# Output projection in token groups of 800 and 256 instead of 704 and 352, the first group's rows kept in DRAM until their norm, outputs on two queues

## The chip, the core and the metric

The kernel runs on one core of a Trainium2 chip. A core has five engines that run their own instruction streams and meet at semaphores: TensorE (PE; its weight loads are listed as PEld), VectorE (DVE), ScalarE (ACT), GpSimd (POOL) and SyncE (SP). SyncE, ScalarE and GpSimd can issue DMA transfers, and an engine whose next instruction is a transfer that has to wait holds up everything behind it on that engine. Data lies in DRAM, in SBUF (128 partitions) and in PSUM, eight banks into which TensorE accumulates.

The metric is the device time of one execution in microseconds (us). Three timed runs of the kernel before gave 1811.63, 1812.21 and 1813.61 us.

## The reference

One layer of a decoder trunk for 1024 prompt tokens and 32 sample tokens (8 sequences of 4), 1056 tokens together, with 2048 features:

```python
xn = rms_norm(x, norm_w)
proj = xn @ w_in                       # split into the inputs of four branches
...
mix = jnp.concatenate([y_ml, y_ssd, y_sc, y_rg], axis=-1)
y = x + mix @ w_out                    # (tokens, 2048) @ (2048, 2048)
...
y_prompt = rms_norm(yp, final_norm_w)  # y * rsqrt(mean(y*y) + EPS) * final_norm_w
y_sample = rms_norm(ys, final_norm_w)
```

All is float32. The change concerns the last two steps, the output projection with its residual and the final norm.

## The kernel before

Features lie on partitions, tokens along the free axis. The 2048 features are 16 tiles of 128 (`KT`), so an output tile `n` is 128 features by a number of tokens.

**Products.** Each float32 operand is split into a high part rounded to the fast matmul format and the rest. `mm6` (line 276) does, for each of the two 128-row slices of a weight pair, three matmuls into one bank: high by high, high by low, low by high (lines 281 to 283). A weight pair is 128 x 256 floats, 128 KiB in DRAM. It is loaded by SyncE into a raw buffer (`w_load`, line 251), ScalarE writes the high part (line 262), VectorE the rest (line 263). In the output projection there are six raw buffers, and a load into one waits for the split that read it last. There are four buffers for split pairs and, in the second token group, four more that lie in `xl`. `w_next` hands out the next split pair, frees the one before it, splits as many as there are free buffers, and loads as many as there are free raw buffers.

**Order.** The program order of each engine is that of the Python code. Work beside the main loop runs in generators on two lanes; `tick()`, called once for each weight pair, lets each lane go one step, and a generator that yields 4 is called again four ticks later. SBUF outside the fixed tiles is one arena, `take` and `drop` give and return areas, and an area that was returned may be handed out at once: whatever then writes it waits for the last reader.

**Output projection (`out_proj`).** The tokens go through in two groups, `GA` and `GB`: 704 tokens as two chunks of 352, then the last 352. In each group all 16 output tiles are computed, so all weights of `w_out` are read twice. The first four tiles of group one go weight by weight through all eight banks, since the inputs still arrive; after that a tile uses two banks of four. `begin(n, gr)` loads the residual x for the tile on SyncE (line 1339). `fin(n, gr, banks)` adds the bank to it (VectorE, line 1349), squares it (ScalarE, 1356) and adds the square to the running sum `acc` (GpSimd, or VectorE for the last two tiles, 1357). In group two it also multiplies by the final norm's weight (1359).

**Final norm of group one (`finish`).** All 16 tiles of group one stay in SBUF, 16 x 704 floats a partition. When the group is done, `finish` is put on a lane and runs beside the second group: `row_rsqrt` turns `acc` into the reciprocal root for each token, spread over the partitions, and then every four ticks a tile is multiplied by it (VectorE, 1452) and written out by GpSimd (1453).

**The end.** After the last matmul of group two the sums over features are made by small matmuls (1421, 1426), roots and reciprocals follow, the reciprocals are spread by transposes (1432), and the 16 tiles are multiplied, eleven by VectorE from PSUM (1441), four by GpSimd (1439), the last by VectorE (1437). SyncE issues all 16 output transfers (1442).

Of the kernel before, what the change touches and what calls it, by code (L numbers as in the profile page):

```python
# [9 lines left out]
F32 = mybir.dt.float32  # L10
# [3 lines left out]
OP = mybir.AluOpType  # L14

D = 2048
KT = 16
TP = 1024
TS = 32
NT = TP + TS  # L20
# [3 lines left out]
NEG = -1e30  # L24
KSC = 128.0 ** -0.5
SLOT = 1084
GA = (CH, CH)
GB = CH
WARM = 12
CM = max(*GA, GB)  # L30

# [77 lines left out]
class Build:  # L109
    def __init__(self, ctx, tc, io):  # L110
        self.tc, self.nc, self.io = tc, tc.nc, io
        nc = tc.nc
        self.V, self.S, self.G, self.P, self.Q = nc.vector, nc.scalar, nc.gpsimd, nc.tensor, nc.sync
        main = ctx.enter_context(tc.tile_pool(name="main", bufs=1))
        psum = ctx.enter_context(tc.tile_pool(name="psum", bufs=1, space=bass.MemoryType.PSUM))
        dram = ctx.enter_context(tc.tile_pool(name="dram", bufs=1, space=bass.MemoryType.DRAM))
        ctx.enter_context(tc.manual_schedule())
        self.xh = main.tile([128, KT, NT], F32R, name="xh")
        self.xl = main.tile([128, KT, NT], F32R, name="xl")
        self.NRAW, self.NW = 3, 4  # L120
        self.wbuf = {}
        self.wraw = deque(main.tile([128, 2, 128], F32, name=f"wr{i}") for i in range(self.NRAW))
        self.whl = deque((main.tile([128, 2, 128], F32R, name=f"wh{i}"), main.tile([128, 2, 128], F32R, name=f"wl{i}"))
                         for i in range(self.NW))
        self.wcur = {}
        self.fa = main.tile([128, 1040], F32R, name="fa")
        self.fb = main.tile([128, 256], F32R, name="fb")
        na = 15290
        self.ar = Arena(main.tile([128, na], F32, name="arena"), na)
        self.bank = [psum.tile([128, 512], F32, name=f"bank{i}") for i in range(8)]  # L130
        self.npj = self.nmx = 0
        self.mixd = dram.tile([KT, 128, NT], F32, name="mixd")
        self.rowd = dram.tile([24, NT], F32, name="rowd")
        self.nrmd = dram.tile([4, NT], F32, name="nrmd")
        self.lanes = [deque(), deque()]
        self.wait = [0, 0]
        self.ready = {}
        self.land = {}
        self.held = False
# [1180 lines left out]
    def out_proj(self):  # L1320
        V, S, G, P, Q = self.V, self.S, self.G, self.P, self.Q
        io = self.io
        W = [sum(GA), GB]
        T0 = [0, W[0]]
        acc = [self.take(W[0]), None]
        ys = [{}, {}]
        sq = [self.take(CM) for i in range(2)]
        nacc = [0, 0]
        nsq = 0
        pairs = lambda ap: ap.rearrange("p (k m) -> p k m", k=2)  # L1330
        for _ in range(3):
            self.wraw.append(pairs(self.take(256).ap))

        def begin(n, gr):
            if gr:
                ys[1][n] = self.take_tick(GB).ap
            else:
                ys[0][n] = self.ar.take(W[0])
            Q.dma_start(ys[gr][n][:, :], io["x"][:, n, T0[gr] + 1:T0[gr] + W[gr] + 1])

        def fin(n, gr, banks):

            nonlocal nsq
            y, a = ys[gr][n], acc[gr]
            o = 0
            nacc[gr] += 1
            for b, w in banks:
                ts = slice(o, o + w)
                V.tensor_add(y[:, ts], b[:, :w], y[:, ts])  # L1349
                o += w  # L1350
                if nacc[gr] == 1:
                    S.activation(a[:, ts], y[:, ts], AF.Square)
                else:
                    t = sq[nsq % 2][:, :w]
                    nsq += 1
                    S.activation(t, y[:, ts], AF.Square)  # L1356
                    (G if nacc[gr] < KT - 1 else V).tensor_add(a[:, ts], a[:, ts], t)  # L1357
                if gr:
                    S.activation(y, y, AF.Copy, scale=self.par("fnorm", n))

        def chunks(gr):
            t = T0[gr]
            out = []
            for w in (GA if gr == 0 else (GB,)):
                out.append((self.pj(), t, w))
                t += w
            return out

        def mm(ch, ke, w):
            for b, t, n in ch:  # L1370
                self.mm6(b, *w, ke, t, n, ke == 0, ke == 7)


        first = [chunks(0) for _ in range(2)] + [[(self.bank[b + i], sum(GA[:i]), w) for i, w in enumerate(GA)] for b in (4, 6)]
        for ke in range(8):
            for n in self.FIRST:
                mm(first[n], ke, self.w_next())
                k = 2 * ke + 6 + n // 2
                if n % 2:
                    if k + 4 < KT:  # L1380
                        self.mix_load(k + 4)
                    if k < KT:
                        self.mix_split(k)
                if ke == 5:
                    begin(n, 0)
                self.tick()
        for n in self.FIRST:
            fin(n, 0, [(b, w) for b, _, w in first[n]])
        self.states_out()
        for n in range(4, KT):  # L1390
            begin(n, 0)
            ch = chunks(0)
            for ke in range(8):
                mm(ch, ke, self.w_next())
                self.tick()
            fin(n, 0, [(b, w) for b, _, w in ch])
        acc[1] = self.take(GB).ap
        self.lanes[0].append(self.finish(acc[0], ys[0]))

        for i in range(4):  # L1400
            self.whl.append((self.xl[:, 2 * i:2 * i + 2, 128:256], self.xl[:, 2 * i + 8:2 * i + 10, 128:256]))
        for n in range(KT):
            begin(n, 1)
            ch = chunks(1)
            for ke in range(8):
                mm(ch, ke, self.w_next())
                self.tick()
            if n == KT - 1:
                break
            fin(n, 1, [(b, w) for b, _, w in ch])  # L1410

        nb = (GB + 127) // 128
        cut = [(i, slice(128 * i, min(GB, 128 * i + 128)), min(128, GB - 128 * i)) for i in range(nb)]
        tc, rc, mean = self.take(nb), self.take(nb), self.take(2)
        V.memset(mean.ap, 1.0 / D)
        V.memset(tc.ap, 1.0)
        S.activation(rc[:, 0:1], tc[:, 0:1], AF.Sqrt)
        bs, bk = [self.mx() for _ in cut], self.pj()
        y, t, b = ys[1], sq[0], ch[0][0]
        for i, ts, m in cut:  # L1420
            P.matmul(bs[i][:m, 0:1], acc[1][:, ts], mean[:, 0:1], start=True, stop=False)
        for ts in (slice(0, 128), slice(128, GB)):
            V.tensor_add(y[KT - 1][:, ts], b[:, ts], y[KT - 1][:, ts])
            S.activation(t[:, ts], y[KT - 1][:, ts], AF.Square)
        for i, ts, m in cut:
            P.matmul(bs[i][:m, 0:1], t[:, ts], mean[:, 0:1], start=False, stop=True)
        for i, ts, m in cut:
            S.activation(tc[:m, i:i + 1], bs[i][:m, 0:1], AF.Sqrt, bias=self.eps[:m])
        V.reciprocal(rc.ap, tc.ap)
        bk2 = self.pj()  # L1430
        for b, (i, ts, m) in [(b, x) for b in (bk, bk2) for x in cut]:
            P.transpose(b[:, ts], rc[:m, i:i + 1].to_broadcast([m, 128]), self.ident[:m, :m])
        rb = self.take(GB)
        S.activation(rb.ap, bk2[:, :GB], AF.Copy)
        for n in range(KT):
            if n == KT - 1:
                V.scalar_tensor_tensor(y[n], y[n], self.par("fnorm", n), rb.ap, op0=OP.mult, op1=OP.mult)
            elif n % 3 == 2 and n < 14:
                G.tensor_mul(y[n], y[n], rb.ap)
            else:  # L1440
                V.tensor_mul(y[n], y[n], bk[:, :GB])
            Q.dma_start(io["y_out"][n, :, W[0]:NT], y[n])

    def finish(self, acc, ys):

        w = acc.n
        yield 4
        rb = self.fa[:, :w].bitcast(F32)
        yield from self.row_rsqrt(acc, w, 1.0 / D, EPS, rb, 3, True)
        for n in range(KT):  # L1450
            y = ys[n]
            self.V.scalar_tensor_tensor(y.ap, y.ap, self.par("fnorm", n), rb, op0=OP.mult, op1=OP.mult)
            self.G.dma_start(self.io["y_out"][n, :, 0:w], y.ap)
            if n:
                ys[n - 1].drop()
            yield 4
        ys[KT - 1].drop()

    def states_out(self):
        G, io = self.G, self.io  # L1460
# [122 lines left out]
```

## Time and profile before

| | |
|---|---|
| median of the timed runs | 1812.21 us |
| the profiled execution | 1812.29 us |
| its span, first to last instruction | 1810.1 us |
| mean granted TensorE clock | 0.995 |
| TensorE busy, weight loads busy | 99%, 97% of the span |
| VectorE, ScalarE, GpSimd busy | 50%, 29%, 10% |
| read from and written to DRAM | 144.35 MB, 21.84 MB |
| first token group's matmuls | to about 1672 us |
| second group's matmuls | to 1795.8 us |

An execution takes about 2.2 us more than its span. In rows that group instructions, the line is followed by engine, operation, output<-inputs, shape and count; behind the bar stand the busy us, the mean ns of one, and the idle us of the engine just before them with what ended them. In the view by windows, each engine's busy us and number of instructions stand for a stretch of the run, then the granted clock, the DMA engines' busy share and GB/s. In the view in order of time a row gives its start in us, its length and how many instructions it merges. Transfer rows give the KiB of one and the median us from issue to landing; in the rows of the DMA queues, q1 is SyncE's queue and q0 GpSimd's, followed by packets, MB, and the share of the sixteen DMA engines' time.

### The profile page before, as it was taken

Reading aid. Unit: us, or ns where it says so; the run is one execution under the profiler, and the core shown is the slowest. Engines: PE = TensorE matmul, PEld = TensorE weight load, DVE = VectorE, ACT = ScalarE, POOL = GpSimd, SP = SyncE. Lnnn points to the kernel's source line nnn. Section 1 sums busy time; section 2 is a strip of 40 time slices with the busy share of each in tenths; the row PEclk is TensorE's granted clock in tenths of the full one; section 3 lists DMA queues with packets and bytes.
Section 4 is the critical chain, followed back from the end, with each engine's and each line's share of the span. In section 5 each row is a group of like instructions: output and inputs, shape, how many; then the busy total and the mean of one; then the engine's idle time right before and its main releaser. Section 6 shows DMA issues by size and latency. Waiting matters only on the chain.

```text
span 1810.1 us, 30156 instructions
## 1 busy us (share of the span) xinstructions
PE 1788.5 (99%) x11459; PEld 1755.0 (97%) x11459; DVE 909.0 (50%) x2018; ACT 529.9 (29%) x1263; POOL 178.8 (10%) x243
## 2 busy tenths in 40 slices
PE   9999999999999999999999999999999999999997
PEld 7899999999999999989999999999999999999997
DVE  4484544625435444764267647543773543333664
ACT  5522222212212111321144212311441432222453
POOL 1000102011011000320000003100000011110121
PEclk9999999999999999999999999999999999999998
DMA  9411213222122112332211224221213633333774
GB/s 321 161 51 50 77 49 91 50 73 71 58 68 62 55 56 71 94 76 81 61 45 57 62 65 107 66 84 53 62 56 95 201 109 99 92 91 87 212 244 153
DMA packets 141557, 168.17 MB, mean 93 GB/s; under 512 B 18220, under 2 KB 126196, under 8 KB 140900
## 3 DMA queue, kind: packets, MB, share of 16 engines
q1 hardware_dynamic: 135492, 145.36, 28.5%
q0 software_dynamic: 5184, 19.42, 2.8%
q8 instruction: 89, 1.46, 0.3%
q10 hardware_dynamic: 736, 1.48, 0.3%
q14 instruction: 56, 0.46, 0.1%
HBM read 144.35 MB, written 21.84 MB: 92 GB/s over the span
## 4 chain that ended last, share of the span: by engine, by line
PE 91%; DMA 4%; DVE 2%; issue 1%; ACT 1%; POOL 1%; SPq 1%; DVEq 0%; POOLq 0%; ACTq 0%
PE bank L281 29%; PE bank L283 29%; PE bank L282 28%; DMA arena<-rowd 3%; POOL arena L1074 1%; DMA wr<-in_w_in 1%; DVE arena L1083 0%; DMA arena<-in_x 0%; DVE wl L263 0%; PE bank L898 0%; PE bank L494 0%; PE bank L876 0%; PE bank L897 0%; PE bank L900 0%; ACT wh L262 0%
## 5 line engine op out<-in xcount | busy, mean ns | idle before, releaser
L281 PE MATMUL bank<-xh,wh 128*128 128x352 f32 x3328 | 1085.6, 326 | 1.4 <-ACT xh L470 0.9
L282 PE MATMUL bank<-xl,wh 128*128 128x352 f32 x3328 | 1072.8, 322 | 2.0 <-DVE xl L473 1.9
L283 PE MATMUL bank<-xh,wl 128*128 128x352 f32 x3328 | 1072.9, 322 | 0.7 <-DVE wl L263 0.5
L281 PEld LDWEIGHTS bank<-xh,wh 128*128 128x128 f32 x3328 | 626.0, 188 | 14.4 <-issue 9.9
L282 PEld LDWEIGHTS bank<-xl,wh 128*128 128x128 f32 x3328 | 626.8, 188 | 3.0 <-DVE xl L473 3.0
L283 PEld LDWEIGHTS bank<-xh,wl 128*128 128x128 f32 x3328 | 626.6, 188 | 2.0 <-DVE wl L263 2.0
L263 DVE TENSOR_TENSOR wl<-wr,wh 128x256 fp32r<-128x256 f32 x537 | 233.1, 443 | 397.9 <-ACT wh L262 397.5
L262 ACT ACTIVATE wh<-wr 128x256 fp32r<-128x256 f32 x537 | 214.6, 412 | 585.4 <-PE bank L282 483.6
L591 DVE TENSOR_TENSOR arena<-bank,arena 128x352 f32<-128x352 f32 x114 | 58.8, 524 | 80.1 <-PE bank L283 79.7
L263 DVE TENSOR_TENSOR wl<-arena,wh 128x256 fp32r<-128x256 f32 x103 | 43.7, 442 | 61.0 <-ACT wh L262 60.9
L1357 POOL TENSOR_TENSOR arena<-arena 128x352 f32<-128x352 f32 x39 | 36.9, 950 | 314.0 <-ACT arena L1356 208.5
L942 DVE SCALAR_TENSOR_TENSOR arena<-arena 128x1080 f32<-128x1080 f32 (+1 forms) x44 | 59.9, 1361 | 1.0
L262 ACT ACTIVATE wh<-arena 128x256 fp32r<-128x256 f32 x103 | 40.3, 410 | 65.4 <-PE bank L282 62.1
L1356 ACT ACTIVATE arena<-arena 128x352 f32<-128x352 f32 x44 | 21.9, 500 | 69.2 <-DVE arena L1349 67.3
L283 PE MATMUL bank<-xh,xl 128*128 128x352 f32 x128 | 41.6, 325 | 0.0
L281 PE MATMUL bank<-xh,xl 128*128 128x352 f32 x128 | 41.6, 325 | 0.0
L282 PE MATMUL bank<-xl 128*128 128x352 f32 x128 | 41.1, 321 | 0.0
L1349 DVE TENSOR_TENSOR arena<-bank,arena 128x352 f32<-128x352 f32 x47 | 24.0, 522 | 32.7 <-PE bank L283 23.9
L584 DVE TENSOR_TENSOR arena<-bank,arena 128x352 f32<-128x352 f32 x32 | 16.3, 521 | 41.5 <-PE bank L283 41.5
L398 DVE RECIPROCAL arena<-arena 128x352 f32<-128x352 f32 (+3 forms) x18 | 35.6, 1981 | 0.2
L473 DVE SCALAR_TENSOR_TENSOR xl<-arena,xh 128x1056 fp32r<-128x1056 f32 (+1 forms) x20 | 21.8, 1096 | 25.6 <-ACT xh L470 25.4
L930 POOL COPY arena<-arena 128x3 f32<-128x3 f32 (+1 forms) x16 | 3.0, 188 | 296.1 <-DVE arena L586 296.1
(339 smaller groups left out, 1253.3 us busy)
## 6 DMA issues: line engine op xcount, KB each, us to landing
wr<-in_w_in SPq DMA_DIRECT2D x438, 128.0 KB, 2.2
wr<-in_w_out SPq DMA_DIRECT2D x130, 128.0 KB, 2.5
arena<-in_w_out SPq DMA_DIRECT2D x126, 128.0 KB, 2.7
arena<-in_xr SPq DMA_DIRECT2D x16, 512.0 KB, 8.1
arena<-rowd SPq DMA_DIRECT2D x32, 256.0 KB, 5.7
mixd<-arena POOLq DMA_DIRECT2D x15, 528.0 KB, 3.9
arena<-mixd SPq DMA_DIRECT2D x15, 528.0 KB, 4.1
arena<-in_x SPq DMA_DIRECT2D x14, 528.5 KB, 7.7
```

What stands on the lines that cost most here:

```text
L262: self.S.activation(h, r, AF.Copy)
L263: self.V.tensor_sub(l, r, h.bitcast(F32))
L281: self.P.matmul(bank[:, :n], wh[:, k, :], xh, start=first and k == 0, stop=False)
L282: self.P.matmul(bank[:, :n], wh[:, k, :], xl, start=False, stop=False)
L283: self.P.matmul(bank[:, :n], wl[:, k, :], xh, start=False, stop=last and k == 1)
L398: self.V.reciprocal(x[:, a:b], x[:, a:b])
L473: V.scalar_tensor_tensor(self.xl[:, k, ts], x, w, self.xh[:, k, ts].bitcast(F32), op0=OP.mult, op1=OP.subtract)
L591: V.tensor_mul(a[:, t0:t0 + CH], bank[:, :CH], rs[:, t0:t0 + CH])
L942: V.scalar_tensor_tensor(y[:, :n], a[:, i:i + n], w(i), y[:, :n], op0=OP.mult, op1=OP.add)
L1349: V.tensor_add(y[:, ts], b[:, :w], y[:, ts])
L1356: S.activation(t, y[:, ts], AF.Square)
L1357: (G if nacc[gr] < KT - 1 else V).tensor_add(a[:, ts], a[:, ts], t)
```

## The change

Three things change, all in the output projection.

- The groups are 800 tokens, as two chunks of 400, and 256 tokens.
- A finished tile of group one is written to a DRAM tensor `yd` by GpSimd as the last act of `fin`, and its area is returned at once. `finish` now loads a tile back on SyncE, two steps before it multiplies it, and returns its area right after the issue of the output transfer. It takes 18 steps of four ticks instead of 16.
- At the end the output transfers of the odd tiles are issued by ScalarE, those of the even tiles by SyncE.

```diff
-GA = (CH, CH)
-GB = CH
+GA = (400, 400)
+GB = 256
...
+        self.yd = dram.tile([KT, 128, sum(GA)], F32, name="yd")
...
                 if gr:
                     S.activation(y, y, AF.Copy, scale=self.par("fnorm", n))
+            if not gr:
+                G.dma_start(self.yd[n], y.ap)
+                y.drop()
...
-        self.lanes[0].append(self.finish(acc[0], ys[0]))
+        self.lanes[0].append(self.finish(acc[0]))
...
-            Q.dma_start(io["y_out"][n, :, W[0]:NT], y[n])
-
-    def finish(self, acc, ys):
+            (S if n % 2 else Q).dma_start(io["y_out"][n, :, W[0]:NT], y[n])
+
+    def finish(self, acc):
...
         yield from self.row_rsqrt(acc, w, 1.0 / D, EPS, rb, 3, True)
-        for n in range(KT):
-            y = ys[n]
-            self.V.scalar_tensor_tensor(y.ap, y.ap, self.par("fnorm", n), rb, op0=OP.mult, op1=OP.mult)
-            self.G.dma_start(self.io["y_out"][n, :, 0:w], y.ap)
-            if n:
-                ys[n - 1].drop()
+        ys = {}
+        for n in range(KT + 2):
+            if n < KT:
+                ys[n] = self.take(w)
+                self.Q.dma_start(ys[n].ap, self.yd[n])
+            if n >= 2:
+                y = ys.pop(n - 2)
+                self.V.scalar_tensor_tensor(y.ap, y.ap, self.par("fnorm", n - 2), rb, op0=OP.mult, op1=OP.mult)
+                self.G.dma_start(self.io["y_out"][n - 2, :, 0:w], y.ap)
+                y.drop()
             yield 4
-        ys[KT - 1].drop()
```

How the rows move is seen at three places. First SyncE in the second group, while `finish` runs. Before, it issues weight loads and, once in eight, an x load (`in_x`); in brackets is what a row waits for: `DMAHW` a transfer that SyncE or ScalarE issued, `DMASW` one that GpSimd issued, an engine's name that engine.

```order
L1339 DMA arena<-in_x 128x352 [waits DMASW6_49]
L251 DMA wr_69<-in_w_out 128x256 [waits DMAHW2_49,DVE_49]
L251 DMA wr_67<-in_w_out 128x256 [waits DMAHW3_49,DVE_49]
L251 DMA wr_68<-in_w_out 128x256 [waits DMAHW4_49,DVE_49]
L251 DMA arena<-in_w_out 128x256 [waits DMAHW5_49,DVE_49]
```

After, at the same stage; the first row loads output tile 4 back:

```order
L1458 DMA arena<-yd 128x800 [waits DMAHW1_49,DMASW7_49]
L252 DMA wr_68<-in_w_out 128x256 [waits DMAHW2_49,DVE_49]
L252 DMA arena<-in_w_out 128x256 [waits DMAHW3_49,DVE_49]
L1340 DMA arena<-in_x 128x256 [waits DMAHW4_49]
L252 DMA arena<-in_w_out 128x256 [waits DMAHW5_49,DVE_49]
L252 DMA arena<-in_w_out 128x256 [waits DMAHW6_49,DVE_49]
L1458 DMA arena<-yd 128x800 [waits DMAHW7_49,DMASW0_49]
L252 DMA wr_69<-in_w_out 128x256 [waits DMAHW0_49,DVE_49]
L252 DMA wr_67<-in_w_out 128x256 [waits DMAHW1_49,DVE_49]
L252 DMA wr_68<-in_w_out 128x256 [waits DMAHW2_49,DVE_49]
```

Every four or so weight loads there is now a read of `yd`, and from tile 4 on it names a GpSimd transfer: the output of the tile three before it (the outputs take the numbers 6, 7, 0, 1 and so on), whose area it takes over.

Second VectorE at the same stage after the change, from the product of tile 1 (L1461) on; L264 is a split, L1350 the add of a bank:

```order
L1461 SCALAR_TENSOR_TENSOR arena<-arena,fa 128x800
L264 TENSOR_TENSOR wl_71<-arena,wh_70 128x256
L264 TENSOR_TENSOR wl_73<-arena,wh_72 128x256
L264 TENSOR_TENSOR wl_75<-wr_69,wh_74 128x256
L264 TENSOR_TENSOR xl<-wr_67,xl 128x2x128
L1461 SCALAR_TENSOR_TENSOR arena<-arena,fa 128x800
L264 TENSOR_TENSOR xl<-wr_68,xl 128x2x128
L264 TENSOR_TENSOR xl<-arena,xl 128x2x128
L1350 TENSOR_TENSOR arena<-bank_83,arena 128x256
L264 TENSOR_TENSOR xl<-arena,xl 128x2x128
L264 TENSOR_TENSOR wl_77<-arena,wh_76 128x256
L1461 SCALAR_TENSOR_TENSOR arena<-arena,fa 128x800
```

The weights that SyncE loads right behind the read of tile 4 go into `wr_68` once the split of `wr_68` above has read it. They are read by the third split behind the last row shown, which is the eleventh behind the first row.

Third the last transfers. Before, SyncE issues sixteen, behind its last weight loads:

```order
L1339 DMA arena<-in_x 128x352
L251 DMA arena<-in_w_out 128x256 x2
L251 DMA wr_69<-in_w_out 128x256
L251 DMA wr_67<-in_w_out 128x256
L1339 DMA arena<-in_x 128x352
L1442 DMA out_y_out<-arena 128x352 x16
```

After, ScalarE's last rows; the roots (L1432) and the copy of the reciprocals (L1438) stand ahead of its transfers:

```order
L1428 ACTIVATE arena<-arena 128x128 x2
L1432 ACTIVATE arena<-bank_87,arena 128x1
L1432 ACTIVATE arena<-bank_85,arena 128x1
L1438 ACTIVATE arena<-bank_84 128x256
L1446 DMA out_y_out<-arena 128x256 x8
```

Eight of the sixteen have gone from SyncE to ScalarE.

## The prediction

> **What bounds the kernel now.** I read the totals first, then the chain that ended last, then one stage at a time.
>
> ```profile
> PE 1788.5 (99%) x11459; PEld 1755.0 (97%) x11459; DVE 909.0 (50%) x2018; ACT 529.9 (29%) x1263; POOL 178.8 (10%) x243
> ...
> PE 91%; DMA 4%; DVE 2%; issue 1%; ACT 1%; POOL 1%; SPq 1%; DVEq 0%; POOLq 0%; ACTq 0%
> ```
>
> TensorE carries 91% of the chain, so a microsecond counts only if it changes the time between matmuls, makes TensorE wait, or lies behind its last matmul. The diff touches only the output projection, which the view by windows splits: the first group of tokens (1440 to 1665 us), the second (1676 to 1790), the second while `finish` runs (1700 to 1760), and, for comparison, the densest transfers of the run (10 to 40).
>
> ```profile
> 10.00:40.00 30.00, 27.71 (x193) 23.44 (x193) 13.16 (x17) 17.72 (x27) 0.00 (x0) 0.94 0.99 346
> 1440.00:1665.00 225.00, 224.48 (x1404) 224.19 (x1404) 76.61 (x156) 66.13 (x153) 26.64 (x30) 1.00 0.35 100
> 1676.00:1790.00 114.00, 114.00 (x707) 113.00 (x704) 67.30 (x164) 57.54 (x149) 21.18 (x29) 1.00 0.71 214
> 1700.00:1760.00 60.00, 60.00 (x371) 59.38 (x370) 38.74 (x86) 29.53 (x76) 14.34 (x21) 1.00 0.80 253
> ```
>
> The last three numbers are the granted clock, the busy share of the DMA engines and GB/s. The first group runs at 225/1404 = 0.1603 us a matmul with transfers at 0.35. The second runs at 114/707 = 0.1612 us, TensorE does not wait, but in `finish` the DMA engines are already 0.80 busy at 253 GB/s; 346 GB/s came with 0.99 busy. ScalarE's groups in 1700 to 1760 show how near that is:
>
> ```profile
> L262 ACT ACTIVATE xl<-wr 128x256 fp32r<-128x256 f32 x17 | 7.0, 414 | 11.0 <-DMA wr<-in_w_out 9.7 <-PE bank L282 1.3
> L262 ACT ACTIVATE xl<-arena 128x256 fp32r<-128x256 f32 x14 | 5.7, 415 | 5.5 <-DMA arena<-in_w_out 5.2 <-PE bank L283 0.2
> ```
>
> ScalarE splits weights 0.41 us at a time and waits for their landing, 9.7 + 5.2 us of 60. TensorE is spared by the pairs split ahead.
>
> **Part 1: widths.** The matmuls stay 16 x 8 x 12 = 1536 in the first group and 16 x 8 x 6 = 768 in the second. Their start times by width:
>
> ```profile
> 541.03 0.32 PE L283 MATMUL bank<-xh,wl 128*128 128x352 f32 x1
> 541.19 0.65 PE L841 MATMUL bank<-fa,fb 96*128 96x390 f32 x3
> 541.67 0.33 PE L281 MATMUL bank<-xh,wh 128*128 128x352 f32 x1
> ...
> 746.75 0.40 PE L1091 MATMUL bank<-fb,fa 96*128 96x256 f32 x2
> 746.99 0.33 PE L281 MATMUL bank<-xh,wh 128*128 128x352 f32 x1
> ```
>
> Two of 256 columns take 0.24 us, 0.120 each. The three of L841 are two of 390 and one of 260 columns: 0.48 - 0.12 leaves 0.18 for 390. No row has 400. The line through 256 and 352, 0.42 ns a column, gives 0.1805; the line from 352 to 390 goes on to 0.185. I take 0.183, nearer the 390 row. First group 1536 x (0.183 - 0.1603) = +35 us, second 768 x (0.120 - 0.1612) = -32: **+3 us**, bounds -1 and +7.
>
> The Trainium skill, "TensorE: Matmul & The Clock Gate", section "Back-to-back issue gap", has N/2.4 + 2.5 ns for a warm matmul, by which the two groups cancel to 0. It gives 149 ns at 352 columns where the trace has 160, so I keep the rows.
>
> **Part 2: rows through DRAM, first group.** Each output adds a 400 KiB write to `yd`; 8 weight pairs, 400 KiB of x and that write are 1.87 MB in 8 x 12 x 0.183 = 17.6 us, 106 GB/s against 100 now. On SyncE the next x load now waits for the write of the output before. Behind it wait the weight loads, on which ScalarE's and VectorE's splits depend. What the write itself follows, by the page's groups:
>
> ```profile
> L1357 POOL TENSOR_TENSOR arena<-arena 128x352 f32<-128x352 f32 x39 | 36.9, 950 | 314.0 <-ACT arena L1356 208.5
> ...
> L1349 DVE TENSOR_TENSOR arena<-bank,arena 128x352 f32<-128x352 f32 x47 | 24.0, 522 | 32.7 <-PE bank L283 23.9
> ...
> wr<-in_w_out SPq DMA_DIRECT2D x130, 128.0 KB, 2.5
> ```
>
> Two adds on VectorE of 0.59 us, two on POOL of 1.08 (both scaled to 400 columns) and a landing of 4.1 (Part 3) make about 7.5 us. Six raw and three split pairs cover 9 x 2.2 = 20 us, so the cost is 0; without that cover, up to 7.5 us an output.
>
> **Part 3: `finish` in the second group.** Here I expect the change to be decided. A weight pair lasts 6 x 0.120 = 0.72 us now instead of 0.97, and `finish` takes one output per four pairs, 2.88 us. In these four: 4 x 128 KiB of weights, half an x load (64), one 400 KiB read of `yd`, one 400 KiB write: 1.409 MB, 489 GB/s. At the 346 GB/s of the row above it takes 4.07 us. Of 18 steps 14 have both read and write: 14 x (4.07 - 2.88) = 16.7 us.
>
> The queues give nearly the same a second way. The rows of 1700 to 1760:
>
> ```profile
> q1 hardware_dynamic: 10228, 9.70, 54.7%
> q0 software_dynamic: 1199, 5.40, 24.2%
> ...
> out_y_out<-arena POOLq DMA_DIRECT2D x14, 352.0 KB, 3.9
> wr<-in_w_out SPq DMA_DIRECT2D x33, 128.0 KB, 3.4
> arena<-in_w_out SPq DMA_DIRECT2D x31, 128.0 KB, 2.9
> ```
> ```profile
> 1725.00 0.95 DVE L1452 SCALAR_TENSOR_TENSOR arena<-arena,fa 128x704 f32<-128x704 f32 x1
> ```
> ```profile
> 1726.25 0.56 POOL L1453 DMA_DIRECT2D out_y_out<-arena  x1 [2.13 <-DVE arena L1452]
> ```
> ```profile
> 1727.92 1.52 SPq L251 DMA_DIRECT2D wr<-in_w_out  x2
> 1730.40 0.33 SPq L1339 DMA_DIRECT2D arena<-in_x  x1
> ```
>
> That x load waits today already, for just this output: 1730.40 - 1726.25 is its landing, 4.1 us. From output 4 on, the read of `yd` waits so for the output three before it, every time. The VectorE product of 800 (0.95 x 800/704 = 1.08 us), 0.30 to POOL's issue, about 4.1 to land, two SyncE issues (0.66), a weight landing (3.2, and 1.2 for the 400 KiB ahead of it in its queue), the split (0.41 + 0.42): 11.4 us. By the order of the rows (VectorE's are shown with the change), eleven splits lie between the product and the split that reads those weights, 7.9 us at TensorE's pace. The loop runs at 11.4/11 x 4 = 4.1 us an output: 12 x (4.1 - 2.88) = 15 us. It is the same time seen from the other side, not a second cost. Taking 17 and subtracting the three or so split pairs in hand when `finish` starts, 2 us, I take **+15 us**.
>
> Bounds: the lower has 372 GB/s (queue 0: 5.40 MB in 24.2% of 60 us), 14 x 0.91 = 12.7, less a full stock of 13 pairs, 9.4 us: +3. The upper has queue 1's 9.70 MB in 54.7%, 296 GB/s, for its 1.00 MB and 372 for the 0.41: 4.48 us, 14 x 1.6 = +22. VectorE, four splits at 0.42, 1.08 and half an add, comes to some 2.95 us a step: full, but below 4.1.
>
> **Part 4: between the groups.** The last add of the first group is done late:
>
> ```profile
> 1669.38 0.53 DVE L1349 TENSOR_TENSOR arena<-bank,arena 128x352 f32<-128x352 f32 x1 [2.16 <-PE bank L283]
> ...
> 1672.00 0.53 DVE L1357 TENSOR_TENSOR arena<-arena 128x352 f32<-128x352 f32 x1 [0.57 <-ACT arena L1356]
> 1672.44 0.42 DVE L263 TENSOR_TENSOR wl<-wr,wh 128x256 fp32r<-128x256 f32 x1
> ```
>
> 3.1 us pass without a split; three pairs ahead, 2.9 us, cover them today. At 0.72 us they cover 2.2, and 400 columns lengthen the 3.1: **+1 us** (0 to +2).
>
> **Part 5: the tail.**
>
> ```profile
> 1795.63 0.32 PE L283 MATMUL bank<-xh,wl 128*128 128x352 f32 x1
> ```
> ```profile
> 1798.72 4.83 DVE L1441 TENSOR_TENSOR arena<-arena,bank 128x352 f32<-128x352 f32 x11 [0.61 <-PE bank L1432]
> 1803.47 0.58 DVE L1437 SCALAR_TENSOR_TENSOR arena<-arena 128x352 f32<-128x352 f32 x1
> ```
> ```profile
> 1799.27 7.97 SPq L1442 DMA_DIRECT2D out_y_out<-arena  x16
> ```
>
> SyncE's sixteen issues, 0.50 each, end at 1807.2, 3.2 us after the last product, and the span 2.9 later. With two queues the products decide: eleven at 4.83 x 256/352 = 3.5 and a last 0.45 from about 1798.4, one issue, 2.9: 1805.8, a gain of 4.3. But 16 x 128 KiB at 346 GB/s need 6.1 us from 1799 on, then land: a gain of about 3. I take **-3.5 us** (-2 to -4.5).
>
> **Sum.** 3 + 0 + 15 + 1 - 3.5 = +15.5. The profiled run took 1812.29 us, 2.2 around its span of 1810.1, and the median is 1812.21: **1828 us**. The bounds' sums are -2.5 and +29.
>
> **Rivals.** (a) *Faster: the transfers keep up.* If reads of 3200-byte rows pass so easily that a step's 1.41 MB fit into 2.9 us (489 GB/s, or the loop's two landings in 5.0 us instead of 8.5), Part 3 vanishes: -1 + 0 - 4 = 1807 us. For it: TensorE does not wait today. Against: ScalarE waits 15 of 60 us at half that rate. Chance 0.08.
> (b) *The stock covers most.* 372 GB/s and thirteen pairs in hand: 3 + 3 + 1 - 4 = 1815 us. The pool of buffers is for it, the thin stock after Part 4 against. Chance 0.12. The Trainium skill, "DMA: Bandwidth & Descriptors", section "Specifications", puts the fabric's ceiling at 435 GB/s and HBM's for one core at about 358; the higher one would lead here as well, and no row here comes near it.
> (c) *Landings stretch.* Engines that are full make each landing of the loop longer; at 1.4 times, 14.8 us for eleven pairs, 5.4 us a step, 12 x 2.5 = 30, less 2: 1841 us. Weight loads land in 2.5 us over the whole projection and in 3.4 at 0.80 busy, which speaks for it; against it, a slower loop also asks for less, and 4.07 us a step is where the rate stops rising. Chance 0.2.
> (d) *The second queue saves nothing,* since both share the DMA engines: tail -2, inside the forecast.
>
> The forecast, 1818 to 1836, has 0.6. Range 1811 to 1843: (c) is partly in it, (a) out. A change under 0.2%, 3.6 us, cannot be told from none here: faster 0.08, same 0.12, slower 0.8.
>
> **What would show it.** Right: the second group's window shows TensorE waiting on splits, ScalarE on weight DMAs, SyncE on `out_y_out` at the read of `yd`, and about 345 GB/s with engines near 0.95. The first group holds 0.183 us a matmul without waits. The tail from the last projection matmul is near 11 us instead of 14.5. Wrong: second group at 0.120 us throughout; 400 columns outside 0.180 to 0.186; or waits in the first group.

## The result, and the profile after

| | before | after |
|---|---|---|
| median of the timed runs | 1812.30 us | 1851.32 us |
| lowest to highest, 4 runs each | 1811.63 to 1813.61 | 1849.74 to 1853.03 |
| span of the profiled execution | 1810.1 us | 1848.0 us |
| first group, first matmul to the second group's first | 246.5 us | 281.5 us |
| second group, from its first matmul to the start of its last | 125.5 us | 130.5 us |
| tail, start of the last matmul to the end of the span | 14.5 us | 13.4 us |

The ratio is 1.0215, 95% interval 1.0203 to 1.0227: slower by 39 us, where 15.5 were forecast. The last three rows are worked out from the start times of the matmuls in the two traces, where the second group's first matmul starts at 1670.1 us before and at 1704.0 after. With -1.1 us that lie ahead of the first group they make up the 37.9 us of the spans: -1.1, +35.0, +5.0, -1.0. By the forecast's terms the second group should have fallen by 16 us (-32 for the narrower matmuls, +15, +1). It rose by 5. That is the whole surprise, but for 2.5 us in the tail.

The view by windows of the changed kernel, for the first group, the second, and 40 us inside `finish`; the columns are those of before:

```profile
1440.00:1700.00 260.00, 258.69 (x1420) 258.31 (x1419) 80.90 (x156) 68.49 (x155) 36.98 (x45) 1.00 0.37 113
1704.00:1830.00 126.00, 107.33 (x739) 94.13 (x739) 70.65 (x170) 57.97 (x153) 18.79 (x30) 0.97 0.80 250
...
1740.00:1780.00 40.00, 31.75 (x201) 26.80 (x200) 22.34 (x47) 16.38 (x42) 7.74 (x13) 0.95 0.93 301
```

The first group runs through: 260/1420 = 0.183 us a matmul. In the second, TensorE is busy 107 of 126 us, and inside `finish` 32 of 40, where before it was busy all the time. 201 matmuls in 40 us are 4.78 us for a step of `finish` (24 matmuls, four weight pairs), where 4.07 were forecast and 2.88 is TensorE's own pace. The DMA engines carry 301 GB/s at 0.93 busy, not the forecast 345 at 0.95.

The view of waits, 1712 to 1800 us (engine, its line, what it waited for: us in total, times, longest):

```profile
PEld bank L282 <- ACT xl L263: 16.1, 17, 2.1
PE bank L282 <- ACT xl L263: 12.5, 15, 1.9
ACT xl L263 <- DMA wr<-in_w_out: 11.8, 9, 3.0
ACT xl L263 <- DMA arena<-in_w_out: 7.6, 7, 2.7
```

TensorE waits for ScalarE's splits, and ScalarE for raw weights that have not landed. The same view for SyncE's queue, 1704 to 1830 us:

```profile
SPq L252 <- DVE xl L264: 20.9, 23, 5.8
SPq L252 <- DVE wl L264: 18.2, 25, 1.7
SPq L1340 <- DMA out_y_out<-arena: 10.7, 5, 4.4
SPq L1458 <- DMA out_y_out<-arena: 9.6, 6, 3.2
```

Two kinds of wait stand here. L1340 (the load of x) and L1458 (the read of `yd`) wait for an output of the first group to leave, as foretold. L252, the weight load, waits 39 us in all for VectorE to finish a split: for one of the six raw buffers to come free. That wait is not new; before, it was longer and harmless (1672 to 1795 us):

```profile
SPq L251 <- DVE wl L263: 38.9, 38, 3.2
SPq L251 <- DVE xl L263: 24.3, 34, 5.1
```

But it says that loads were already issued only as buffers came free, and ScalarE's waits on landings in the prediction's rows say that no landed weights lay in reserve. The forecast had no term for that. What landings take there, from the view of transfers, 1712 to 1800 us:

```profile
arena<-yd SPq DMA_DIRECT2D x15, 400.0 KB, 4.5
out_y_out<-arena POOLq DMA_DIRECT2D x14, 400.0 KB, 5.1
arena<-in_w_out SPq DMA_DIRECT2D x40, 128.0 KB, 3.7
wr<-in_w_out SPq DMA_DIRECT2D x39, 128.0 KB, 5.1
```

The tail, in order of time:

```profile
1834.54 0.28 PE L284 MATMUL bank<-xh,wl 128*128 128x256 f32 x1
...
1837.67 5.10 SPq L1446 DMA_DIRECT2D out_y_out<-arena  x8
1837.94 2.78 POOL L1443 TENSOR_TENSOR arena<-arena 128x256 f32<-128x256 f32 x4 [11.29 <-ACT arena L1438]
1838.00 5.15 ACTq L1446 DMA_DIRECT2D out_y_out<-arena  x8
```

All outputs are issued by 1843.15, 5.5 us after the first (8.0 before), and still the span ends only at 1847.96. The last output packet ended at 1844.97. What holds the end is a closing drain instruction on GpSimd, which the trace records and the views do not list: it returns at 1847.18, 6.46 us after GpSimd's last product, and the 0.8 us behind it hold only the program's closing instructions.

### The profile page after: what moved, and what is told of

Read it like the earlier page. It is cut to its first block, busy times and chain, and to the rows that moved or that the text cites. A ratio compares the mean times of both kernels' runs of the same rounds, so it can differ in the third digit from the quotient of the medians.

```text
span 1848.0 us, 30212 instructions
## 1 busy us (share of the span) xinstructions
PE 1805.9 (98%) x11453; PEld 1760.6 (95%) x11453; DVE 910.8 (49%) x2018; ACT 529.9 (29%) x1262; POOL 185.8 (10%) x259
## 4 chain that ended last, share of the span: by engine, by line
PE 86%; DMA 7%; DVE 3%; ACT 2%; issue 1%; POOL 1%; SPq 0%; DVEq 0%; ACTq 0%; POOLq 0%
PE bank L282 27%; PE bank L284 27%; PE bank L283 27%; DMA arena<-rowd 2%; DMA arena<-in_w_out 2%; DMA wr<-in_w_out 1%; DVE wl L264 1%; DMA arena<-in_x 1%; DMA wr<-in_w_in 1%; DVE arena L1084 0%; POOL arena L1075 0%; ACT xl L263 0%; ACT wh L263 0%; PE bank L495 0%; PE bank L899 0%
## 5 line engine op out<-in xcount | busy, mean ns | idle before, releaser
L282 PE MATMUL bank<-xh,wh 128*128 128x352 f32 (+2 forms) x3328 | 1091.8, 328 | 3.0 <-ACT wh L263 1.8
L284 PE MATMUL bank<-xh,wl 128*128 128x352 f32 (+2 forms) x3328 | 1079.6, 324 | 2.1 <-DVE wl L264 1.9
L283 PE MATMUL bank<-xl,wh 128*128 128x352 f32 (+2 forms) x3328 | 1078.4, 324 | 1.9 <-DVE xl L474 1.9
L264 DVE TENSOR_TENSOR wl<-wr,wh 128x256 fp32r<-128x256 f32 x537 | 234.4, 446 | 420.4 <-ACT wh L263 416.1
L592 DVE TENSOR_TENSOR arena<-bank,arena 128x352 f32<-128x352 f32 x114 | 58.6, 523 | 81.3 <-PE bank L284 80.9
L264 DVE TENSOR_TENSOR wl<-arena,wh 128x256 fp32r<-128x256 f32 x103 | 44.6, 447 | 77.4 <-ACT wh L263 74.4
L1358 POOL TENSOR_TENSOR arena<-arena 128x400 f32<-128x400 f32 (+1 forms) x39 | 36.7, 945 | 202.0 <-ACT arena L1357 201.4
L282 PE MATMUL bank<-xh,xl 128*128 128x256 f32 x128 | 39.0, 305 | 16.3 <-ACT xl L263 16.2
L282 PEld LDWEIGHTS bank<-xh,xl 128*128 128x128 f32 x128 | 24.4, 191 | 21.7 <-ACT xl L263 21.0
L1350 DVE TENSOR_TENSOR arena<-bank,arena 128x400 f32<-128x400 f32 (+1 forms) x47 | 24.1, 524 | 36.6 <-PE bank L284 34.0
L1357 ACT ACTIVATE arena<-arena 128x400 f32<-128x400 f32 (+1 forms) x44 | 22.0, 501 | 68.6 <-DVE arena L1350 65.9
L284 PE MATMUL bank<-xh,xl 128*128 128x256 f32 x128 | 39.0, 305 | 0.0
L585 DVE TENSOR_TENSOR arena<-bank,arena 128x352 f32<-128x352 f32 x32 | 16.3, 521 | 41.5 <-PE bank L284 41.5
L283 PE MATMUL bank<-xl 128*128 128x256 f32 x128 | 36.4, 284 | 0.0
```

The source lines that it names most:

```text
L264: self.V.tensor_sub(l, r, h.bitcast(F32))
L282: self.P.matmul(bank[:, :n], wh[:, k, :], xh, start=first and k == 0, stop=False)
L283: self.P.matmul(bank[:, :n], wh[:, k, :], xl, start=False, stop=False)
L284: self.P.matmul(bank[:, :n], wl[:, k, :], xh, start=False, stop=last and k == 1)
L592: V.tensor_mul(a[:, t0:t0 + CH], bank[:, :CH], rs[:, t0:t0 + CH])
```

## The experiments

Three explanations stood against each other for the second group. *Volume*: the DMA engines carry only some 300 GB/s of this mix. *SyncE's waits*: the loads queued behind the waiting reads of `yd` come late. *Raw buffers*: six 128 KiB buffers are too few when a weight pair lasts 0.72 us instead of 0.97. All times below but those of the timed pairs are single runs, and the projection begins anywhere from 1422.5 to 1428.4 us in their traces. So the length of the second group in each trace, measured as in the table above, says more than the time. It has a scatter too: e10, whose second group does the same work as the changed kernel's, differs from it by 1.2 us. Diffs are against the changed kernel unless they say otherwise.

| run | time, us | second group, us |
|---|---|---|
| changed kernel | 1851.32 | 130.5 |
| e1_ring | 1847.77 | 125.1 |
| e3_raw12 | 1843.57 | 118.5 |
| e4_ring_raw12 | 1831.68 | 112.6 |
| e2_no_finish | 1824.93 | 105.9 |
| e9_no_finish_raw12 | 1814.96 | 93.7 |
| e8_half_bytes | 1835.96 | 116.5 |
| e5_old_widths | 1824.11 | 135.8 |
| e12_old_ring6_raw12 | 1812.33 | 124.7 |
| e10_yd_on_act | 1848.29 | 129.3 |

**e1_ring: reads of `yd` into eight areas of their own,** so that neither they nor the loads of x wait for an output.

```diff
+        self.ring = [self.take(W[0]) for _ in range(8)]
         self.lanes[0].append(self.finish(acc[0]))
...
-                ys[n] = self.take(w)
+                ys[n] = self.ring[n % 8]
...
-                y.drop()
```

> The rows come back into a ring of eight areas, so no read of yd and no x load waits for an output transfer that was just issued (SyncE waited 10.7 + 9.6 us for those). Theory W (SyncE's waits for output landings make the weights late): most of the 39 us that the second group loses goes, 1851 falls to about 1831, and the transfers then reach some 345 GB/s. Theory B (the volume is over what the DMA engines carry, 296 to 303 GB/s at 0.92 to 0.95 busy): under 6 us, 1845 to 1851. Theory L (six raw buffers and landings of 5.1 us give one weight pair in about 1.05 us at best): under 6 us as well.

Measured: 1847.77 us, second group 5.4 us shorter. The window 1740 to 1780:

```profile
1740.00:1780.00 40.00, 32.83 (x226) 28.30 (x225) 23.03 (x49) 18.43 (x46) 8.01 (x13) 1.00 0.97 322
```

SyncE no longer waits for `out_y_out` anywhere in the second group, yet TensorE still waits, as volume and raw buffers both had it. The loop through SyncE that the prediction worked out is real and worth 5.4 us, not most of the loss. At this point volume seemed the better theory.

**e2_no_finish: without read, product and output of the first group's rows** (these outputs are not written).

```diff
-        for n in range(KT + 2):
+        for n in range(0):
```

> finish stops after the reciprocal roots: nothing is read back, multiplied or written, so the first group's output rows are left unwritten (they are still written to yd). It measures what the second group costs without finish. If all of the loss is finish, the second group lasts 768 x 0.120 = 92 us and the time falls to about 1812. If 256 columns alone already outrun the weights (0.72 us a pair against six buffers whose cycle is a landing of 2.5 to 3.1 us, a wait for SyncE and a split of 0.85, together some 4.1 to 4.6 us, 0.68 to 0.77 us a pair) the second group lasts 95 to 105 us and the time is 1815 to 1825.

Measured: 1824.93 us. The second group still takes 105.9 us, though 768 matmuls at the 0.1185 us that the trace of e9 shows for 256 columns (48 in 5.69 us) are 91. Its weight loads land sooner than the changed kernel's (view of transfers, 1712 to 1800 us):

```profile
wr<-in_w_out SPq DMA_DIRECT2D x55, 128.0 KB, 3.0
arena<-in_w_out SPq DMA_DIRECT2D x54, 128.0 KB, 2.6
```

So some 15 us are lost with no `finish` and little traffic beside the weights, 2.3 of them in the first eight weight pairs, at the boundary of the groups.

**e8_half_bytes: `finish` reads, multiplies and writes 400 of its 800 tokens** (the other half is not written).

```diff
-                self.Q.dma_start(ys[n].ap, self.yd[n])
+                self.Q.dma_start(ys[n][:, :w // 2], self.yd[n][:, :w // 2])
...
-                self.V.scalar_tensor_tensor(y.ap, y.ap, self.par("fnorm", n - 2), rb, op0=OP.mult, op1=OP.mult)
-                self.G.dma_start(self.io["y_out"][n - 2, :, 0:w], y.ap)
+                self.V.scalar_tensor_tensor(y[:, :w // 2], y[:, :w // 2], self.par("fnorm", n - 2), rb[:, :w // 2], op0=OP.mult, op1=OP.mult)
+                self.G.dma_start(self.io["y_out"][n - 2, :, 0:w // 2], y[:, :w // 2])
```

> finish reads back, multiplies and writes only 400 of the 800 tokens of each tile (the others are left unwritten); number and order of the transfers and all waits stay. The volume of a step of four pairs falls from 1.41 to 1.00 MB. Theory B: at about 300 GB/s a step takes 3.3 instead of 4.7 us, and some 20 us go: about 1830. Theory W: a landing falls only from 5.1 to about 4 us, two of them in a loop of eleven pairs, 2.2 of 13 us: 5 us go, about 1846, if the landings do not depend on the load. Theory L: the same as W.

Measured: 1835.96 us, between the two expectations; second group 116.5. Halving the bytes takes 14.0 of the 24.6 us that lie between the changed kernel and e2. Bytes matter (the product on VectorE is halved with them). But a step now moves 1.00 MB, which would fit into 2.9 us at 346 GB/s, and 10.6 us are still left.

**e3_raw12: twelve raw weight buffers instead of six.**

```diff
-        for _ in range(3):
+        for _ in range(9):
             self.wraw.append(pairs(self.take(256).ap))
```

> Twelve raw weight buffers instead of six in the output projection. Theory L: landings of 5.1 us are covered, the loss in finish (28 us) falls by half or more: under 1838. Theory W: the loop from product over output landing, read and weight landing to the split now spans 17 pairs instead of 11, the same 13 us give 0.76 us a pair: under 1835. Theory B: the stock of loaded weights grows by six pairs, 4 us: about 1846.

Measured: 1843.57 us, second group 12.0 us shorter. The time meets none of the three expectations; its projection begins 5.8 us later than the changed kernel's. Outside `finish` and behind the first eight pairs, eight weight pairs (48 matmuls) take 5.66 to 5.84 us by the starts of the matmuls (5.69 at TensorE's own pace, changed kernel 6.1 to 8.3); inside `finish` they still take 6.6 to 10.7, most of them 8 and more.

**e9_no_finish_raw12: e2 with twelve raw buffers.**

> The changed kernel without the read back, the product and the writes of the first group (as in e2_no_finish, whose second group took 105.9 us where 768 matmuls at 119.5 ns are 92 us), and with 12 raw weight buffers in place of 6. If six buffers that each come free only after a landing and a split are what holds the second group above the matmuls' own pace, it falls to about 94 us (2 us at the boundary stay) and the run to 1813 to 1815. If it is held by something else that stays (the order of the splits on ScalarE, the boundary), it stays near 105 us and 1825.

Measured: 1814.96 us, second group 93.7. The window 1740 to 1780 of e2, then that of e9:

```profile
1740.00:1780.00 40.00, 39.67 (x309) 37.48 (x310) 21.90 (x60) 23.35 (x65) 4.49 (x6) 1.00 0.65 189
```
```profile
1740.00:1780.00 40.00, 40.00 (x340) 40.00 (x339) 23.35 (x63) 25.35 (x72) 5.39 (x8) 1.00 0.76 215
```

With six buffers the engines are 0.65 busy, and still TensorE does 309 matmuls instead of 340. With twelve the same program asks for more, gets it, and runs at TensorE's pace. So 12.2 of e2's 15 us are the raw buffers; the 2.3 us at the boundary stay.

**e4_ring_raw12: both easings, `finish` complete.**

> The changed kernel with both easings at once: read-backs into eight areas of their own, so that SyncE waits for no output, and 12 raw weight buffers. If the volume is what binds (32 MB in the second group at the 306 GB/s that e1_ring showed are 105 us), the second group stays at 105 to 118 us and the run at 1834 to 1842. If SyncE's waits and the six buffers made the loss between them, it comes to 95 to 98 us and the run to 1815 to 1820.

Measured: 1831.68 us, second group 112.6. Windows and landings:

```profile
1740.00:1780.00 40.00, 33.54 (x243) 29.77 (x243) 26.00 (x55) 17.29 (x50) 9.13 (x15) 1.00 1.01 356
```
```profile
arena<-in_w_out SPq DMA_DIRECT2D x73, 128.0 KB, 5.3
arena<-yd SPq DMA_DIRECT2D x16, 400.0 KB, 6.0
out_y_out<-arena POOLq DMA_DIRECT2D x16, 400.0 KB, 6.0
```

The second group lies in the range that volume gave (105 to 118 us), the time 2.3 us below its range, and the reason written for it falls: the engines do not stop at 306 GB/s, they carry 356 here and 345 over 1735 to 1800. A step takes 24 x 40/243 = 3.95 us, against 4.07 forecast. The Trainium skill, "DMA: Bandwidth & Descriptors", section "Specifications", puts HBM's share for one core at about 358 GB/s; e4's 356 over 40 us lies close to it, but over 1740 to 1760 the same trace carries 363, so it is not shown here as a bound.

What TensorE waits for has changed in e4. From its view of waits, 1712 to 1800 us:

```profile
ACT arena L1357 <- DVE arena L1350: 43.1, 11, 4.7
DVE arena L1462 <- DMA arena<-yd: 11.7, 10, 2.3
ACT xl L263 <- DMA arena<-in_w_out: 0.7, 1, 0.7
```

The weights are there in time. VectorE's product now waits for its read of `yd`, the add of a bank behind it comes late, and ScalarE, whose next instruction squares what that add wrote, stands still for up to 4.7 us with the following splits behind it. So the 18.9 us by which e4 exceeds e9 are the price of `finish`, but that the rate of the DMA engines sets them is argued from the busy share of 1.01, not shown: a read issued more than two steps ahead was not run.

The five runs form one account of the second group. Twelve buffers take 12.0 us off the changed kernel and 12.2 off it without `finish`; the ring takes 5.4 off with six buffers and 5.9 with twelve. The parts simply add: 93.7 without either loss or `finish`, +18.9 for `finish` with both easings (e4 - e9), +12 for the raw buffers, +6 for SyncE's waits, which is the changed kernel's 130.5 but for 0.1.

**e5_old_widths: the detour through DRAM and the two output queues, at 704 and 352 tokens.**

```diff
-GA = (400, 400)
-GB = 256
+GA = (CH, CH)
+GB = CH
```

> The changed kernel at the old widths, 704 and 352 tokens, with the detour through DRAM and the two output queues. If the volume binds: a step of four pairs lasts 3.87 us at the matmuls' pace and moves 1.335 MB, 345 GB/s, where some 306 are carried, so 14 steps lose about 7 us less what the buffers hold; no loss before and after them; 1814 to 1820. If the detour costs by its waits whatever the widths are, 1825 or more. If it costs nothing here, 1811 to 1813.

Measured: 1824.11 us, between the two expectations; second group 135.8, 10.3 more than before. A miss for volume: inside `finish`, from 1705 to 1745, the engines were 0.88 busy (first row below), so they were not full, and still TensorE waited.

**e12_old_ring6_raw12: e5 with twelve raw buffers and a ring of six areas.**

> The changed kernel at the old widths, as e5_old_widths (1824.1), with both easings: read-backs into six areas of their own and 12 raw weight buffers. In e4_ring_raw12 the queues carried 345 GB/s, which is what a step at the old widths asks for (1.335 MB in 3.87 us). If the loss of e5 was the buffers' shortness, the detour is free here: 1811 to 1814. If the detour costs by itself (contention, or its place on SyncE's queue), it stays above 1818.

Measured: 1812.33 us beside 1811.89 of the kernel before on the same chip; second group 124.7 us, eight pairs in 7.71 us from the second set to the last. The window of e5, then that of e12:

```profile
1705.00:1745.00 40.00, 37.55 (x224) 35.37 (x222) 21.33 (x45) 17.78 (x43) 9.09 (x13) 1.00 0.88 282
```
```profile
1705.00:1745.00 40.00, 40.00 (x251) 40.00 (x250) 26.24 (x58) 20.89 (x56) 10.99 (x16) 1.00 0.97 335
```

At the old widths the detour is free once loads run far enough ahead: in the same stretch of `finish` the engines carry 335 GB/s instead of 282, and TensorE does not wait. The low rate of e5 came from the waits; it did not cause them. What the detour costs there, 11 us, is all shortness of buffers and the waits on outputs (which of the two, this pair does not tell).

**e10_yd_on_act: ScalarE issues the writes of `yd`,** so that GpSimd issues 62 transfers, as before, not 78.

```diff
-                G.dma_start(self.yd[n], y.ap)
+                S.dma_start(self.yd[n], y.ap)
```

> The changed kernel with the 16 writes of the first group's rows issued by ScalarE in place of GpSimd, so that GpSimd issues 62 transfers as before, not 78. If GpSimd's closing drain sets the end and lasts longer by the transfers that it issued, it is 7.97 us here as in e2_no_finish, and the time 1 to 1.5 us below the changed kernel's, 1849.5 to 1850.5. If the drain's length comes from something else, it stays at 9.27 us and the time at 1851.

Measured: 1848.29 us; tail 12.1 instead of 13.4 us, the drain 7.96 instead of 9.27 us. The tail's 1.3 us are as expected; the time lies 1.2 us below its range, within the scatter of single runs. GpSimd's drain did set the end.

**e6_queues_only: the kernel before with its final outputs on two queues** (diff against before).

```diff
-            Q.dma_start(io["y_out"][n, :, W[0]:NT], y[n])
+            (S if n % 2 else Q).dma_start(io["y_out"][n, :, W[0]:NT], y[n])
```

> The kernel before with its final outputs issued by SyncE and ScalarE in turn; widths and rows as before. By the transfers: 16 outputs of 128 x 352 are 2.88 MB, 8.4 us at 345 GB/s, from the first issue at 1799.3 to 1807.7, where the last issue was at 1806.8 and the span ended at 1810.1; by GpSimd's closing drain the span can't end before about 1809.3. So 0 to 0.8 us are saved: 1811.4 to 1812.3. If issuing on one queue was what the tail cost (7.5 us from first to last issue), half of it goes and the time is near 1808.7.

Measured: 1811.04 us against 1811.89, ratio 0.9998, interval 0.9989 to 1.0007: no difference. The issues, from the view in order of time, and the transfers of 1795 to 1809 us:

```profile
1797.71 6.48 SPq L1442 DMA_DIRECT2D out_y_out<-arena  x8
```
```profile
q1 hardware_dynamic: 1152, 1.44, 28.8%
q10 hardware_dynamic: 1152, 1.44, 28.6%
```

Each queue carried half, and the 2.88 MB took the engines 0.574 x 14 = 8.0 us all the same. From the start of the last matmul to the end of the span it is 14.4 us with two queues and 14.5 with one. At the old widths the outputs' own transfers end the run, not their issue.

**e11_queues_act and e13_queues_act_raw9: can either part be turned to profit?** e11 is e6 with the first group's outputs issued by ScalarE in place of GpSimd; e13 adds three raw buffers (both against before).

```diff
-            self.G.dma_start(self.io["y_out"][n, :, 0:w], y.ap)
+            self.S.dma_start(self.io["y_out"][n, :, 0:w], y.ap)
```

> As e6_queues_only, and the first group's 16 outputs are issued by ScalarE in place of GpSimd, so that GpSimd issues 46 transfers in all. If GpSimd's drain (81 ns for each of the 16 that it issued more, by 9.27 against 7.97 us) sets the end of e6, 1.3 us more come off until the 8.4 us of the transfers set it: 1810.5 to 1811.5. If the transfers set the end already, it equals e6. If ScalarE's issues delay the splits of the second group, slower than e6.

> As e11_queues_act with 9 raw weight buffers in place of 6 (what the space allows). The kernel before goes at the matmuls' pace in its second group (7.71 to 7.73 us for 8 weight pairs) but for the first 8 pairs with 9.24 and one set with 8.12. If the buffers are short there, 1 to 2 us come off e11: 1809 to 1810.5. If the boundary's loss has another cause, it equals e11.

Measured: 1820.10 and 1820.57 us, ratios 1.0044 (1.0032 to 1.0057) and 1.0048 (1.0035 to 1.0060): both slower by under half a per cent, by what was named last for e11. In e11's waits, 1680 to 1790 us:

```profile
PEld bank L281 <- ACT xl L262: 6.8, 9, 1.3
PE bank L281 <- ACT xl L262: 4.3, 8, 1.0
```

TensorE waits for ScalarE, whose queue now holds each output until VectorE's product is done, with the splits behind it: one product ends at 1711.66, the output is issued at 1711.69, the next split starts at 1712.07. The second group grew from 125.0 (e6) to 133.2 us. In e13 the first eight pairs took 7.80 us instead of 9.24, but the pause has only moved ahead of them:

```profile
1672.33 0.32 PE L283 MATMUL bank<-xh,wl 128*128 128x352 f32 x1
1673.45 0.75 PE L308 MATMUL bank<-arena 128*1 128x352 f32 x2 [0.80 <-issue]
1674.93 0.75 PE L308 MATMUL bank<-arena 128*1 128x352 f32 x2 [0.73 <-DVE arena L1357]
1675.61 0.43 PE L281 MATMUL bank<-xh,wh 128*128 128x352 f32 x1
```

3.3 us pass here between the last projection matmul of the first group and the first of the second, where e11 has 0.16 us as between any two matmuls; L308, the small matmuls that start `finish`, only fill the gap. In e12, with twelve buffers, the first eight pairs still take 9.24. So more raw buffers do not remove the boundary's loss.

No version run here beats the kernel before. e6 equals it, and e12 does in a single run.

## Why the prediction was wrong, point by point

**Part 1, +3 us: right.** The first group rose by 35.0 us, as worked out. e9, whose second group has no `finish` and enough buffers, stands at 93.7 us, 31.8 below before, where -32 and +1 (Part 4) were summed.

**Part 2, 0 us: right.** SyncE did wait for the writes of `yd` at the loads of x, 90.5 us in all in the first group, and the six raw and three split pairs hid it: 0.183 us a matmul throughout.

**Part 3, +15 us: the step that failed.** Against e9's 93.7 us, the changed kernel's second group shows 36.8 us in its place. The main term came out near in size: fourteen steps of 4.07 us gave 16.7, and `finish` with both easings cost 18.9 (e4 - e9), at 3.95 us a step in the window shown and 345 GB/s; that the rate sets this is argued, as said at e4. What failed is what was set around it.
- *"It is the same time seen from the other side, not a second cost."* The loop through SyncE's waits is a second cost: the ring that removes it saves 5.4 us, and it saves as much, 5.9, with twelve raw buffers.
- *Subtracting the stock in hand.* There was none to subtract: TensorE waited already ahead of the first read of `yd` (1728 us): behind the boundary eight pairs took 7.1 and 6.6 us instead of 5.69. The forecast counted pairs already split, but not the rate at which six raw buffers can be refilled. In e2 a pair takes 6 x 40/309 = 0.78 us, so a buffer goes round in 6 x 0.78 = 4.7 us: 2.6 to 3.0 for the landing, the rest for the split and the next issue. At 352 columns a buffer has 6 x 0.97 = 5.8 us, and in the kernel before that was enough; at 256 it has 6 x 0.72 = 4.3. That costs 12 us, with `finish` or without.

The sign was there to read: ScalarE's waits on landings, 9.7 + 5.2 of 60 us before, were taken for a sign that the DMA engines were near their limit. At 0.80 busy they were not; ScalarE waited because each load had been issued only when a buffer came free.

**Rival (c), longer landings,** was forecast at 1841 us for a step of 5.4 us; the step is 4.78 and the weights land in 3.7 and 5.1 us. It named the right link (landings inside a loop), but in the loop through SyncE and not in that of the raw buffers, and so put nothing outside `finish`, where 12 of e2's us lie. The upper bound of Part 3, +22, was too low for the same reason: it varied the rate and left out the depth. So the measured time lies outside the range of 1811 to 1843 us (the bounds' sums, -2.5 and +29, give 1810 to 1841). (a) and (b) fell. (d) has e6 for it at the old widths, where the second queue saved nothing.

**Part 4, +1 us: right in size.** With the raw buffers eased (e9), the first eight pairs lose 2.3 us. But the pairs ahead did not cover the pause before, as was assumed: 1.5 us were lost there already (9.24 us instead of 7.71).

**Part 5, -3.5 us: wrong, -1.0.** The issues did shrink from 8.0 to 5.5 us, and the last output packet ended 7.3 us after the first issue, near the sum's 6.1 us and a landing. But GpSimd's drain ends later. It was out of sight before (it returned at 1808.32, the last output packet ended at 1808.70), and the change lengthened it itself by sixteen more transfers on GpSimd's queue. In e10, without them, the tail fell by 2.4 us.

**The forecast's signs.** Waits of TensorE on splits, of ScalarE on weights and of SyncE on outputs all showed. The ones that did not fit were the tail and 301 GB/s instead of 345, and the latter pointed to the fault: engines short of requests, not of speed.

## What to carry to other kernels

When a consumer is made faster, first work out whether its load buffers still go round in time: number of buffers times the time of one use must exceed landing plus conversion plus issue. If a stage already waits on landings with the DMA engines below full, as here at 0.80, suspect the depth; a bandwidth sum says too little. And look at what every engine does at the very end: work moved to a queue can lengthen its closing.

## What the runs showed of the hardware that was not expected

**GpSimd's closing drain grows with the transfers that GpSimd issued.** From the end of GpSimd's last arithmetic instruction to the drain's end the traces have 3.84 us with 46 such transfers (e11, e13), 5.15 with 62 (before, e2, e6, e9, e10) and 6.46 with 78 (the changed kernel, e1, e3, e4, e5, e8, e12): 82 ns for each, whatever else the kernel does and although the transfers themselves had long landed. The count was changed by the kernels' own edits; why a drain should take so long is not shown.

**A high busy share is not yet the full rate.** Inside `finish`, transfers of the same shapes ran at 301 GB/s with the engines 0.93 busy (the changed kernel), 322 at 0.97 (e1) and 356 at 1.01 (e4); at the old widths at 282 with 0.88 (e5) and 335 with 0.97 (e12). The edits between these runs only let loads be issued earlier. That the number outstanding is what raises the rate is inferred from this; it was not counted.
